# Hybrid conv encoder step: the last down product in three stretches of tokens instead of two, and VectorE instead of GpSimd for the output rows of a finished stretch

## The chip, the cores and the metric

One core of a Trainium2 chip runs one program. The metric is the device time of the whole program in microseconds, as the median of several runs. The profile below is of one execution of the same program.

## The reference

An encoder layer with two half-step feed-forward networks around a pair of gated convolution branches, and a norm at the end, over 512 + 64 tokens of 1024 features. What matters here is its last part, cut to the lines that it consists of:

```python
def rms_norm(x, g):
    xf = x.astype(jnp.float32)
    y = xf * lax.rsqrt(jnp.mean(xf * xf, axis=-1, keepdims=True) + EPS)
    return (y * g.astype(jnp.float32)).astype(x.dtype)

def swiglu_ffn(x, w_gate_up, w_down):
    gate, up = jnp.split(x @ w_gate_up, 2, axis=-1)
    return (jax.nn.silu(gate) * up) @ w_down
...
    x = x + 0.5 * swiglu_ffn(rms_norm(x, ffn2_norm), ffn2_w_gate_up, ffn2_w_down)
...
y_prompt = rms_norm(xp, final_norm)
y_sample = rms_norm(xs, final_norm)
```

Everything is float32. The hidden width of the feed-forward network is 2816.

## The kernel before

Features lie on the 128 partitions and the 576 tokens on the free axis, so the residual `X` is 8 tiles of 128 x 576. Every product is made of three matmuls in fp32r, TensorE's one-pass form of float32: a weight tile and an operand are each split into a high part (rounded to fp32r) and a low part (the rest), and high x high, high x low and low x high are added up in PSUM (`mm`). Each matmul has its own 128 x 128 weights. Up to the last stage a product covers the tokens in two halves of 288.

Weights come from HBM by a stream of DMAs on SP's queue into `raw` tiles. ScalarE rounds them to the high part and writes its negative, and a DMA with accumulation on GpSimd's queue (POOL) adds the raw tile to that, which leaves the low part.

The instructions of TensorE, VectorE, ScalarE and GpSimd stay in the order in which the program calls them (`Ordered`, whose line 81 stands at nearly every row of the profile). So the order of the Python code is the order on each engine, and an engine that waits holds up all that stands behind it.

The hidden features are worked off in four groups of tiles. The down product of the last group is the program's last: six hidden tiles, hence 6 x 3 = 18 matmuls for each stretch of tokens and each of the eight feature tiles `j`. The first three feature tiles are done over all tokens. For the other five (`LATE`) the tokens are taken in stretches (`LATE_SPANS`): all five tiles over the first stretch, then all five over the second, with the same weights. After each product

- VectorE adds half of it to `X[j]` (`x<-mm,x` in the profile),
- ScalarE squares the new `X[j]` (`tmp<-x`), and VectorE adds the square to `acc` (`fsum`),
- ScalarE writes `X[j]` times the gain of the final norm into an output tile (`gained`; `g<-x,gains`); an output tile `ys[q]` holds two feature tiles.

When all five tiles of a stretch are done, `rstd` makes the reciprocal root: two matmuls with a matrix of ones add up `acc` over the partitions, VectorE scales the sum (`tmp<-mm`), ScalarE takes the root (`r<-tmp`), and three VectorE steps refine it (`tmp<-r`, `tmp<-tmp,tmp`, `r<-tmp,r`). For a stretch that is not the last, `fsum.gather` first splits `acc` into two fp32r parts; for the last, the two matmuls run in plain float32, on `acc` and on the last square. Then each output tile is multiplied by the root and sent to HBM (`put`).

Before, the first stretch has 304 tokens and the second 272. The root of the first stretch is made right behind the second stretch's first product, and its four multiplies are GpSimd's, while TensorE goes on with the second stretch; those of the second stretch are VectorE's, at the end of the program. Output tiles come from a pool of eight buffers (`gtile`), PSUM tiles from a pool of four (`psum2`).

Of the kernel before, what the change touches and what calls it, by code (L numbers as in the profile page):

```python
# [11 lines left out]
ALU = mybir.AluOpType  # L12

P = 128
D = 1024
KT = D // P
# [5 lines left out]
T = SEQ + DSEQ  # L22
# [20 lines left out]
LATE = range(3, KT)  # L43

HALVES = ((0, H), (H, T))
LATE_SPANS = (((0, 304),), ((304, T),))

FIRST_KS = (1, 1, 2, 2, 2)
WARM = 10
# [55 lines left out]
def tile_encoder_step(  # L105
# [6 lines left out]
    nc = tc.nc  # L112
    pe, dve, sca, pool = (
        Ordered(tc, e, c)
        for e, c in (
            (nc.tensor, pe_cost), (nc.vector, dve_cost), (nc.scalar, None), (nc.gpsimd, None)
        )
    )
# [12 lines left out]
    def nm(s):  # L131
        uid[0] += 1
        return f"{s}_{uid[0]}"
# [4 lines left out]
    def gtile(dt=F32, n=LB):  # L138
        return conv.tile([P, 640], dt, tag="g", name=nm("g"))[:, :n]
# [7 lines left out]
    def ttile(dt=F32):  # L147
        return tmp.tile([P, T], dt, tag="tmp", name=nm("tmp"))

    def psum2():  # L150
        return mmps.tile([P, 2, 512], F32, tag="mm", name=nm("mm"))
# [26 lines left out]
    def table(func):  # L178

        t = cpool.tile([P, 1], F32, tag="table", name=nm("table"))  # L180
        sca.activation(t, eps, func)
# [6 lines left out]
    def par(j, r, n=1):  # L188
        return gains[:, r : r + n, j] if r < R_CA else prm[:, r - R_CA : r - R_CA + n, j]
# [198 lines left out]
    def mm(ps, w, kk, xs, first, last, spans=HALVES, six=SIX):  # L388


        (whi, wlo), (xh, xl) = w, xs
        parts = ((whi, xh), (whi, xl), (wlo, xh))
        for n, s in six:
            if s < len(spans):
                (a, b), (i, e) = parts[n], spans[s]
                pe.matmul(
                    ps[:, s, : e - i], a[:, kk, :], b[:, i:e],
                    start=first and n == 0, stop=last and n == 2,
                )

    def chunks(name):

        got = []
        for n in plan[name]:
            w = ws.get(n)
            got += [(w, kk) for kk in range(ws.units[n][1])]
        return got
# [19 lines left out]
    def product(name, xs, then=None, order=None, got=None):  # L427

        if name in early:
            return early.pop(name)[:, :, :H]  # L430
        ps = psum2()
        if order or got:
            got = got or chunks(name)
            for n, k in enumerate(order or range(len(xs))):
                mm(ps, *got[k], xs[k], n == 0, n == len(xs) - 1)
        else:
            k = 0
            for n in plan[name]:
                w = ws.get(n)
                for kk in range(ws.units[n][1]):  # L440
                    mm(ps, w, kk, xs[k], k == 0, k == len(xs) - 1)
                    k += 1
        take()
        if then is None:
            dve.time = max(dve.time, pe.time)
            return ps[:, :, :H]
        fill()
        behind.append((pe.time, lambda: then(ps[:, :, :H])))

    def both(names, xs):  # L450

        ps = [psum2() for _ in names]
        ws_ = [chunks(name) for name in names]
        for k in range(len(xs)):
            for p, w in zip(ps, ws_):
                mm(p, *w[k], xs[k], k == 0, k == len(xs) - 1)
        return [p[:, :, :H] for p in ps]
# [78 lines left out]
            n = spans[0][1] - spans[0][0]  # L536
            return p[:, :, :n] if len(spans) == 2 else p[:, 0, :n]

    def rstd(total, spans=HALVES):

        a, t = ttile(), ttile()
        r = rpool.tile([P, T], F32, tag="r", name=nm("r"), bufs=2)
        tot = total.total(spans)
        span = slice(spans[0][0], spans[-1][1])
        shaped = halves if len(spans) == 2 else (lambda v: v)
        a, t, y = a[:, span], t[:, span], r[:, span]
        dve.tensor_scalar(shaped(a), tot, 1.0 / D, EPS, op0=ALU.mult, op1=ALU.add)
        sca.activation(y, a, AF.Abs_reciprocal_sqrt)
        dve.scalar_tensor_tensor(t, y, -0.5, y, op0=ALU.mult, op1=ALU.mult)
        dve.tensor_tensor(t, t, a, op=ALU.mult)  # L550
        dve.scalar_tensor_tensor(y, t, 1.5, y, op0=ALU.add, op1=ALU.mult)
        return r
# [151 lines left out]
    table(AF.Abs_reciprocal_sqrt)  # L704
    multiply(7)
    R1 = rstd(ss)
    table(AF.Silu)
    forms1.combine(0)
# [10 lines left out]
    def update(j, ps, R=None):  # L719

        x = halves(X[j])
        if R is None:
            dve.scalar_tensor_tensor(x, ps, 0.5, x, op0=ALU.mult, op1=ALU.add)
        else:
            t = halves(ttile())
            dve.scalar_tensor_tensor(t, ps, 0.5, halves(R), op0=ALU.mult, op1=ALU.mult)
            dve.tensor_tensor(x, x, t, op=ALU.add)

    def ffn(f, xg, sums, finish, forms, R=None, todo=()):
# [5 lines left out]
        def plain(i, hs):  # L735
# [4 lines left out]
            if R is None:  # L740
                R = rstd(sums)
# [220 lines left out]
    for j in range(KT):  # L962
        raw = j < RAW_J
        xs = xg if raw else xn
        product(("p", 4, j), xs, gate_b(j, raw))
        if R is None:
            R = rstd(ss)
        if raw:
            xn.extend(scaled(range(3 * j, min(KT, 3 * j + 3)), R))
        product(("p", 3, j), xs, value_b(j))  # L970
# [165 lines left out]
    def finish2(g, hs):  # L1136
        fsum = Sum()
        table(AF.Abs_reciprocal_sqrt)
        ps = both([("f2", "d", g, j) for j in range(2)], hs)
        for j in range(LATE[0]):  # L1140
            update(j, ps[j] if j < 2 else product(("f2", "d", g, j), hs))
            fsum.square(X[j])
            fsum.add(dve)
        late = {}
        ydst = y.rearrange("(q a p) t -> q p a t", a=2, p=P)

        ys = {}

        def gained(j, span):

            n = span.stop - span.start
            q, a = j // 2, j % 2
            if a == 0:
                ys[q] = gtile(n=2 * n).rearrange("p (a n) -> p a n", a=2)
            sca.activation(ys[q][:, a, :], X[j][:, span], AF.Copy, scale=par(j, R_NF))

        def put(spans, engine, queues):

            i, e = spans[0]
            RF = rstd(fsum, spans)[:, i:e].unsqueeze(1).broadcast_to((P, 2, e - i))  # L1160
            for q in range(KT // 2):
                engine.tensor_tensor(ys[q], ys[q], RF, op=ALU.mult)
                queues[q % 2].dma_start(ydst[q, :, :, i:e], ys[q])

        for n, spans in enumerate(LATE_SPANS):
            i, e = spans[0]
            span = slice(i, e)
            fsum.n = LATE[0]
            for j in LATE:
                if n == 0:  # L1170
                    late[j] = chunks(("f2", "d", g, j))
                ps = psum2()
                for k, (w, kk) in enumerate(late[j]):
                    mm(ps, w, kk, hs[k], k == 0, k == len(hs) - 1, spans)
                xj = X[j][:, span]
                dve.scalar_tensor_tensor(
                    xj, ps[:, 0, : e - i], 0.5, xj, op0=ALU.mult, op1=ALU.add
                )
                if n > 0 and j == LATE[0]:
                    put(LATE_SPANS[0], pool, (nc.sync, nc.sync))  # L1180
                    fsum.terms = None
                fsum.square(X[j], span=span)
                fsum.add(dve)
                if j == LATE[0]:
                    for b in range(LATE[0]):
                        gained(b, span)
                gained(j, span)
            if n == 0:
                fsum.gather(span)
        put(spans, dve, (nc.sync, sca))  # L1190

    ffn("f2", xg, ss, finish2, forms)


# [43 lines left out]
```

## Time and profile before

| | |
|---|---|
| runs shown, median | 1304.97 us (1304.52 to 1306.55, three runs) |
| profiled execution | 1305.16 us, of which the span of its instructions is 1303.4 us |
| TensorE busy | 1287.0 us, 99% of the span |
| VectorE, ScalarE, GpSimd busy | 68%, 59%, 30% of the span |
| chain that ended last | TensorE 96%, VectorE 2%, ScalarE 1%, DMA 1% |
| mean granted TensorE clock | 0.995 |

In the rows of the profile, PE is TensorE's matmuls, PEld its weight loads, DVE VectorE, ACT ScalarE, POOL GpSimd, SP SyncE. A row of the timeline has the start and the duration in us, the engine, the line, the operation, what is written and read, the shape, a count, and in brackets the idle time before it with who ended it. A row of a group has the count, then the busy time in us and the mean of one in ns, then the idle time before. A row that merges several instructions runs from the first one's start to the last one's end. Matmuls are pipelined: one of them is shown longer than the time after which the next one starts. Plain float32 matmuls and their loads show twice for each one in the program.

### The profile page before, as it was taken

How to read it: one execution, taken by the hardware profiler on the slowest of the kernel's cores; microseconds unless marked ns; L12 is line 12 of the kernel's file. 1: busy time of each engine (PE TensorE's matmuls, PEld its weight loads, DVE VectorE, ACT ScalarE, POOL GpSimd, SP SyncE). 2: the span in 40 equal slices, each digit the busy share in tenths (PEclk: the TensorE clock that was granted, in tenths of full speed). 3: DMA queues.
4: the chain of work that ended last, by engine and by line, in shares of the span. 5: the costliest groups of instructions: out<-in, count | busy, mean ns of one | idle time of the engine just before them, and what ended most of it. 6: DMA issues, size and time to landing. Idle time of an engine off the chain costs nothing.

```text
span 1303.4 us, 25701 instructions
## 1 busy us (share of the span) xinstructions
PE 1287.0 (99%) x9754; PEld 1284.8 (99%) x9754; DVE 890.4 (68%) x1463; ACT 771.5 (59%) x1365; POOL 388.7 (30%) x487
## 2 busy tenths in 40 slices
PE   9899999999999999999999999999999999999997
PEld 9899999999999999999999999999999999999996
DVE  6748758747945899888885260336967848847955
ACT  7755646645677654555544684457665655654664
POOL 0142332332242554333321322222142141241233
PEclk9899999999999999999999999999999999999999
DMA  6596796796798898878885978776687696796784
GB/s 195 122 181 157 143 192 151 163 197 144 157 189 183 164 213 175 168 170 176 172 170 124 198 159 177 158 162 143 139 172 170 148 195 151 162 204 137 161 177 108
DMA packets 287804, 215.91 MB, mean 166 GB/s; under 512 B 15552, under 2 KB 250048, under 8 KB 287680
## 3 DMA queue, kind: packets, MB, share of 16 engines
q0 software_dynamic: 59472, 97.81, 45.9%
q1 hardware_dynamic: 226336, 115.33, 31.2%
q8 instruction: 77, 1.26, 0.4%
q10 hardware_dynamic: 1872, 1.13, 0.3%
q14 instruction: 47, 0.39, 0.1%
HBM read 113.81 MB, written 2.62 MB: 89 GB/s over the span
## 4 chain that ended last, share of the span: by engine, by line
PE 96%; DVE 2%; ACT 1%; DMA 1%; issue 0%; DVEq 0%; SPq 0%; ACTq 0%
PE mm L81 96%; DVE acc L81 0%; DVE tmp L81 0%; DMA raw<-in_ffn_w_gate_up_dram 0%; ACT tmp L81 0%; ACT act L81 0%; DMA x<-in_x_dram 0%; DVE act L81 0%; ACT w L81 0%; DVE g L81 0%; DVE x L81 0%; ACT L81 0%; DVEq L1228 0%; DVE r L81 0%; ACT u L81 0%
## 5 line engine op out<-in xcount | busy, mean ns | idle before, releaser
L81 PE MATMUL mm<-act,u 128*128 128x288 f32 x4686 | 660.5, 294 | 0.0
L81 PEld LDWEIGHTS mm<-act,u 128*128 128x128 f32 x4686 | 630.9, 188 | 0.2 <-DMA u<-raw 0.2
L81 PE MATMUL mm<-act,g 128*128 128x288 f32 x2778 | 401.6, 295 | 5.4 <-DVE tmp L81 5.4
L81 PEld LDWEIGHTS mm<-act,g 128*128 128x128 f32 x2778 | 380.1, 189 | 5.9 <-ACT g L81 4.8
L81 PE MATMUL mm<-act,act 128*128 128x288 f32 (+2 forms) x2244 | 306.2, 293 | 0.6 <-ACT act L81 0.6
L81 PEld LDWEIGHTS mm<-act,act 128*128 128x128 f32 x2244 | 297.4, 188 | 0.8 <-ACT act L81 0.8
L81 POOL DMA_DIRECT2D u<-raw x200 | 174.8, 874 | 371.5 <-ACT u L81 306.4
L81 ACT CAST u<-raw 128x512 fp32r<-128x512 f32 (+2 forms) x203 | 116.2, 572 | 158.8 <-PE mm L81 128.2
L81 POOL DMA_DIRECT2D g<-raw x123 | 107.7, 875 | 315.5 <-ACT g L81 226.2
L81 DVE SCALAR_TENSOR_TENSOR w<-g,prm,w 128x606 f32<-128x606 f32 x232 | 179.3, 843 | 1.4 <-ACT w L81 1.4
L81 DVE TENSOR_TENSOR tmp<-mm,tmp 128x288 f32<-128x288 f32 (+1 forms) x239 | 107.7, 459 | 76.8 <-PE mm L81 58.9
L81 POOL DMA_DIRECT2D act<-raw x90 | 78.0, 866 | 198.7 <-ACT act L81 191.7
L81 ACT ACTIVATE u<-u 128x512 fp32r<-128x512 f32 (+2 forms) x200 | 118.6, 593 | 6.3
L81 ACT CAST g<-raw 128x512 fp32r<-128x512 f32 (+2 forms) x126 | 68.9, 547 | 41.2 <-DMA raw<-in_ffn_w_down_dram 19.3
L81 DVE SCALAR_TENSOR_TENSOR tmp<-mm,r 128x576 f32<-128x576 f32 x48 | 36.3, 757 | 76.5 <-PE mm L81 76.5
L81 ACT CAST u<-w 128x512 fp32r<-128x512 f32 x79 | 48.9, 619 | 63.5 <-DVE w L81 56.3
L81 ACT CAST g<-w 128x512 fp32r<-128x512 f32 x77 | 47.7, 620 | 59.7 <-DVE w L81 53.6
L81 ACT CAST act<-tmp 128x576 fp32r<-128x576 f32 x84 | 56.7, 675 | 42.3 <-DVE tmp L81 40.8
L81 DVE TENSOR_TENSOR act<-tmp,act 128x576 fp32r<-128x576 f32 x84 | 62.2, 755 | 19.3 <-ACT act L81 17.9
L81 ACT ACTIVATE g<-g 128x512 fp32r<-128x512 f32 (+2 forms) x123 | 69.8, 568 | 3.9
L81 ACT CAST act<-raw 128x512 fp32r<-128x512 f32 (+3 forms) x94 | 55.6, 592 | 10.7 <-PE mm L81 7.5
L81 DVE TENSOR_TENSOR w<-raw,raw 128x512 f32<-128x512 f32 x78 | 53.4, 685 | 12.3 <-DMA raw<-in_ffn_w_gate_up_dram 12.3
(89 smaller groups left out, 808.2 us busy)
## 6 DMA issues: line engine op xcount, KB each, us to landing
raw<-in_ffn_w_gate_up_dram SPq DMA_DIRECT2D x171, 256.0 KB, 3.4
u<-raw POOLq DMA_DIRECT2D x141, 256.0 KB, 4.0
raw<-in_w_in_dram SPq DMA_DIRECT2D x112, 256.0 KB, 3.9
act<-raw POOLq DMA_DIRECT2D x80, 256.0 KB, 4.0
raw<-in_ffn_w_down_dram SPq DMA_DIRECT2D x96, 192.0 KB, 3.5
g<-raw POOLq DMA_DIRECT2D x64, 256.0 KB, 3.9
u<-raw POOLq DMA_DIRECT2D x43, 192.0 KB, 4.7
g<-raw POOLq DMA_DIRECT2D x43, 192.0 KB, 4.5
```

The costliest lines, as they stand in the source:

```text
L81: return self.tc.keep_in_program_order(fn(*args, **kwargs))
```

## The change

The tokens of the last five products are taken in three stretches of 272, 208 and 96. The multiplies by the root are VectorE's in every stretch. `put` returns them as a list of steps, one for each output tile; they are taken one by one behind VectorE's steps of the next stretch. The root of a finished stretch is made one product later for each stretch (`j == LATE[n]`): behind the second product of the second stretch, and behind the third one of the third. Steps that are left over when the last root is made are put between its scaling and its refinement (`meanwhile`).

```diff
-LATE_SPANS = (((0, 304),), ((304, T),))
+LATE_SPANS = (((0, 272),), ((272, 480),), ((480, T),))
...
-    def rstd(total, spans=HALVES):
+    def rstd(total, spans=HALVES, meanwhile=()):
...
         sca.activation(y, a, AF.Abs_reciprocal_sqrt)
+        for step in meanwhile:
+            step()
         dve.scalar_tensor_tensor(t, y, -0.5, y, op0=ALU.mult, op1=ALU.mult)
...
-        def put(spans, engine, queues):
+        def put(spans, ys, queues, meanwhile=()):
 
             i, e = spans[0]
-            RF = rstd(fsum, spans)[:, i:e].unsqueeze(1).broadcast_to((P, 2, e - i))
-            for q in range(KT // 2):
-                engine.tensor_tensor(ys[q], ys[q], RF, op=ALU.mult)
-                queues[q % 2].dma_start(ydst[q, :, :, i:e], ys[q])
+            RF = rstd(fsum, spans, meanwhile)[:, i:e].unsqueeze(1).broadcast_to((P, 2, e - i))
+
+            def rows(q, v):
+                dve.tensor_tensor(v, v, RF, op=ALU.mult)
+                queues[q % 2].dma_start(ydst[q, :, :, i:e], v)
+
+            return [(lambda q=q, v=v: rows(q, v)) for q, v in ys.items()]
+
+        puts = []
 
         for n, spans in enumerate(LATE_SPANS):
             i, e = spans[0]
             span = slice(i, e)
             fsum.n = LATE[0]
+            done = dict(ys)
             for j in LATE:
...
-                if n > 0 and j == LATE[0]:
-                    put(LATE_SPANS[0], pool, (nc.sync, nc.sync))
+                if n > 0 and j == LATE[n]:
+                    puts.extend(put(LATE_SPANS[n - 1], done, (nc.sync, nc.sync)))
                     fsum.terms = None
+                elif puts and j == LATE[-1]:
+                    puts.pop(0)()
                 fsum.square(X[j], span=span)
                 fsum.add(dve)
...
                 gained(j, span)
-            if n == 0:
+                if puts and j > LATE[n]:
+                    puts.pop(0)()
+            if n < len(LATE_SPANS) - 1:
                 fsum.gather(span)
-        put(spans, dve, (nc.sync, sca))
+        for rows in put(spans, ys, (nc.sync, sca), puts):
+            rows()
```

On TensorE, where the root of the first stretch is made: `mm_...` are PSUM tiles, `act_...` weight parts and hidden features, `ones_r` the matrix of ones and `tmp_...` the two parts of the gathered squares. Before, at the end of the second stretch's first product:

```order
L81 MATMUL mm_16225<-act_15910,act_15924 128x272
L81 MATMUL mm_16225<-act_15908,act_15925 128x272
L81 MATMUL mm_16248<-tmp_16220,ones_r 128x304
L81 MATMUL mm_16248<-tmp_16221,ones_r 128x304
L81 MATMUL mm_16273<-act_15180,act_15931 128x272
L81 MATMUL mm_16273<-act_15198,act_15931 128x272
```

Now, at the end of its second product:

```order
L81 MATMUL mm_16254<-act_15910,act_15938 128x208
L81 MATMUL mm_16254<-act_15908,act_15939 128x208
L81 MATMUL mm_16277<-tmp_16220,ones_r 128x272
L81 MATMUL mm_16277<-tmp_16221,ones_r 128x272
L81 MATMUL mm_16290<-act_15180,act_16024 128x208
L81 MATMUL mm_16290<-act_15198,act_16024 128x208
```

The pair has moved behind one more product of 18 matmuls, and all rows around it have 208 columns where they had 272.

On VectorE, the end of the program: `x_94` is the last feature tile, `r_...` the root, `g_...` the output tiles. Before:

```order
L81 SCALAR_TENSOR_TENSOR x_94<-mm_16347,x_94 128x272
L81 TENSOR_SCALAR tmp_16370<-mm_16373 128x272
L81 SCALAR_TENSOR_TENSOR tmp_16371<-r_16372 128x272
L81 TENSOR_TENSOR tmp_16371<-tmp_16371,tmp_16370 128x272
L81 SCALAR_TENSOR_TENSOR r_16372<-tmp_16371,r_16372 128x272
L81 TENSOR_TENSOR g_16267<-g_16267,r_16372 128x544
```

Now:

```order
L81 TENSOR_TENSOR acc_15912<-acc_15912,tmp_16484 128x96
L81 TENSOR_TENSOR g_16248<-g_16248,r_16451 128x416
L81 SCALAR_TENSOR_TENSOR x_94<-mm_16491,x_94 128x96
L81 TENSOR_TENSOR g_16251<-g_16251,r_16451 128x416
L81 TENSOR_TENSOR g_16288<-g_16288,r_16451 128x416
L81 TENSOR_SCALAR tmp_16518<-mm_16521 128x96
L81 TENSOR_TENSOR g_16339<-g_16339,r_16451 128x416
L81 SCALAR_TENSOR_TENSOR tmp_16519<-r_16520 128x96
L81 TENSOR_TENSOR tmp_16519<-tmp_16519,tmp_16518 128x96
L81 SCALAR_TENSOR_TENSOR r_16520<-tmp_16519,r_16520 128x96
L81 TENSOR_TENSOR g_16398<-g_16398,r_16520 128x192
```

Four multiplies of the second stretch stand around the last update: one ahead of it, two between it and the scaling, one between the scaling and the first step of refinement. The steps of the last stretch have 96 columns, and its output tiles 192.

## The prediction

> **What bounds the kernel now.** I read the page's shares and chain first, then the chain and the timeline of the last 40 us, then the groups of instructions there by shape, since all that the change touches lies behind 1267.96 us.
>
> ```profile
> span 1303.4 us, 25701 instructions
> PE 1287.0 (99%) x9754; PEld 1284.8 (99%) x9754; DVE 890.4 (68%) x1463; ACT 771.5 (59%) x1365; POOL 388.7 (30%) x487
> PE 96%; DVE 2%; ACT 1%; DMA 1%; issue 0%; DVEq 0%; SPq 0%; ACTq 0%
> ```
>
> TensorE is 96% of the chain, so a matmul added anywhere lengthens the kernel, and only the part behind the last product is held by other engines. In the timeline of TensorE's matmuls and weight loads (start, duration, operation, count, idle time and who ended it) the last products are these:
>
> ```profile
> 1267.96 14.84 PE L81 MATMUL mm<-act,act 128*128 128x304 f32 x108
> 1282.64 0.85 PE L81 MATMUL mm<-tmp,ones_r 128*128 128x304 f32 x2
> 1283.08 0.19 PEld L81 LDWEIGHTS mm<-tmp,ones_r 128*128 128x128 f32 x1 [0.33 <-DVE tmp L81]
> 1283.18 9.20 PEld L81 LDWEIGHTS mm<-act,act 128*128 128x128 f32 x72
> 1283.32 9.28 PE L81 MATMUL mm<-act,act 128*128 128x272 f32 x72
> L81 PE MATMUL mm<-act,act 128*128 128x272 f32 x90 | 11.7, 289 | 0.0
> ```
>
> The 72 matmuls of 272 columns take 9.28 us; less the 0.29 of a single one, over 71 steps, that is one every 126.6 ns. The x108 row holds the 90 of 304 columns and the 18 of the second stretch's first product: (14.84 - 0.29 - 17 x 0.1266) / 90 = 137.8 ns for one of 304. Between 1282.64 and 1283.32 the two small matmuls of the norm's sum cost 0.68 us, 0.33 of it a wait for VectorE. The last product ends at 1283.32 + 9.28 = 1292.60. What follows is a serial chain:
>
> ```profile
> 1292.77 0.43 DVE L81 SCALAR_TENSOR_TENSOR x<-mm,x 128x272 f32<-128x272 f32 x1
> 1293.29 0.43 ACT L81 ACTIVATE tmp<-x 128x272 f32<-128x272 f32 x1 [1.60 <-DVE x L81]
> 1293.77 0.73 PE L81 MATMUL mm<-tmp,ones 128*128 128x272 f32 x2
> 1294.53 0.44 DVE L81 TENSOR_SCALAR tmp<-mm 128x272 f32<-128x272 f32 x1 [1.34 <-PE mm L81]
> 1295.01 0.43 ACT L81 ACTIVATE r<-tmp 128x272 f32<-128x272 f32 x1 [0.88 <-DVE tmp L81]
> 1295.47 0.44 DVE L81 SCALAR_TENSOR_TENSOR tmp<-r 128x272 f32<-128x272 f32 x1 [0.49 <-ACT r L81]
> 1296.42 0.44 DVE L81 SCALAR_TENSOR_TENSOR r<-tmp,r 128x272 f32<-128x272 f32 x1
> 1296.90 2.63 DVE L81 TENSOR_TENSOR g<-g,r 128x544 f32<-128x544 f32 x4
> 1298.35 1.65 ACTq L81 DMA_DIRECT2D out_y_dram<-g  x2
> ```
>
> From 1292.60 to the span's end it is 10.8 us. Nearly every step of it has the last stretch's 272 tokens as its width; 3.87 us lie behind the last row multiply (1296.90 + 2.63 = 1299.53): issue and landing of the last DMA and the program's end.
>
> **The change part by part.** A third stretch means 90 more matmuls, each with a weight load of its own, and the columns of all stretches together stay 576. What counts is the price of a narrow matmul, which no row shows for these products: the narrowest fp32r one has 272 columns. Weight loads show themselves where TensorE had been idle, or where the matmul is short:
>
> ```profile
> 1283.18 0.19 PEld L81 LDWEIGHTS mm<-act,act 128*128 128x128 f32 x1
> 1292.89 0.30 PEld L81 LDWEIGHTS mm<-acc,ones 128*128 128x128 f32 x2 [0.51 <-DVE acc L81]
> 1293.77 0.30 PEld L81 LDWEIGHTS mm<-tmp,ones 128*128 128x128 f32 x2 [0.57 <-ACT tmp L81]
> 4.46 0.41 PEld L81 LDWEIGHTS mm<-ones 128*128 128x128 f32 x3
> ```
>
> The fp32r load of 1283.08 is followed by the next one at 1283.18, 0.10 us later; two plain loads of 0.19 each take 0.30 together, so they start 0.11 apart. In each case I read the second load's start as the moment when the first set of weights is in place and its matmul begins, with room for one set ahead; a set then takes 0.10 to 0.11 us. The last loads of the warm-up, ahead of matmuls of 128 columns, step by (0.41 - 0.19) / 2 = 0.11 as well. So a matmul with new weights would not follow its forerunner in less than about 0.11 us, however few its columns: at 272 the load hides behind the 126.6 ns of stream, at 208 just no longer, at 96 not at all. The lower bound is 0.104 for 208 columns and 0.065 for 96, by carrying on the line from 304 to 272 (0.35 ns a column); the upper bound is the 126.6 ns of 272. I take 0.11 for both, by the warm-up's steady row, which is nearest: there too each matmul has a load of its own.
>
> [...]
>
> Term 1, first stretch 304 to 272: 90 x (0.1378 - 0.1266) = -1.0.
>
> Term 2, a new wait in it. The last product (j = 7) needs the low parts of its weights, which POOL's accumulating DMAs bring:
>
> ```profile
> 1274.93 1.82 POOL L81 DMA_DIRECT2D act<-raw  x2 [2.21 <-ACT act L81]
> DMA to landing us min/median/max: 3.0/3.1/3.3
> ```
>
> The first of the two lands at 1274.93 + 3.0 = 1277.93, the second, issued 0.96 later, at 1279.2. Before, the first low part is the 75th matmul's, at 1267.96 + 74 x 0.1378 = 1278.16, with its load one step earlier, so 0.1 us of slack. Now that load stands ready at 1267.96 + 73 x 0.1266 = 1277.2, and the DMA comes only some 0.14 earlier (ScalarE, busy all that time, saves 4 x 0.03 on the gained rows, 537 against 508 ns, and 0.02 on the square, 452 against 430, rows below). It waits 0.6, and the second unit, nine matmuls on, another 0.1: +0.7 (from 0 to 0.9).
>
> Term 3, the second stretch 272 to 208: 90 x (0.11 - 0.1266) = -1.5. Term 4, the third stretch: 90 x 0.11 = +9.9. Term 5, the norm's sums: 0.68 before; now two pairs, each one product later, when VectorE has long made their operands, so 0.25 + 0.22, which is -0.2.
>
> Term 6, the tail. Durations by shape in the last stage (busy, mean ns):
>
> ```profile
> L81 DVE SCALAR_TENSOR_TENSOR x<-mm,x 128x576 f32<-128x576 f32 x3 | 2.3, 758 | 6.0 <-PE mm L81 6.0
> L81 DVE SCALAR_TENSOR_TENSOR x<-mm,x 128x272 f32<-128x272 f32 x5 | 2.2, 436 | 0.7 <-PE mm L81 0.6
> L81 DVE TENSOR_TENSOR g<-g,r 128x544 f32<-128x544 f32 x4 | 2.6, 719 | 0.0
> L81 ACT ACTIVATE tmp<-x 128x576 f32<-128x576 f32 x2 | 1.4, 688 | 2.1 <-DVE x L81 2.1
> L81 ACT ACTIVATE tmp<-x 128x304 f32<-128x304 f32 x5 | 2.3, 452 | 2.9 <-DVE x L81 2.9
> L81 ACT ACTIVATE tmp<-x 128x272 f32<-128x272 f32 x5 | 2.1, 430 | 4.3 <-DVE x L81 4.3
> L81 ACT ACTIVATE g<-x,gains 128x304 f32<-128x304 f32 x8 | 4.0, 537 | 0.0
> L81 ACT ACTIVATE g<-x,gains 128x272 f32<-128x272 f32 x8 | 3.8, 508 | 0.0
> L81 DVE TENSOR_TENSOR acc<-acc,tmp 128x272 f32<-128x272 f32 x4 | 3.4, 857 | 1.6 <-ACT tmp L81 1.6
> L81 POOL TENSOR_TENSOR g<-g,r 128x608 f32<-128x608 f32 x4 | 6.4, 1616 | 9.4 <-DVE r L81 9.4
> out_y_dram<-g SPq DMA_DIRECT2D x4, 304.0 KB, 2.3
> out_y_dram<-g ACTq DMA_DIRECT2D x2, 272.0 KB, 2.6
> out_hist_dram<-hst ACTq DMA_DIRECT2D x1, 256.0 KB, 3.4
> ```
>
> VectorE costs some 1.05 ns a column and 0.15 us besides (758 and 436 ns for 576 and 272; 719 for 544), ScalarE 0.85 and 0.20. At 96 columns that is 0.25 and 0.28. The five serial VectorE steps before the rows save 0.18 each (-0.9), the two of ScalarE 0.15 each (-0.3), the sum's two matmuls about 0.26. The four row multiplies go from 544 to 192 elements: 0.35 for one, 0.27 from start to start (they overlap by 0.08: 2.63 is three steps of 0.64 and 0.72), 1.2 in place of 2.63, -1.4. The update x of the last product started 0.17 behind the matmul, since VectorE was in a slowed sum (857 ns in place of some 440 while POOL multiplies): -0.1, as POOL has no multiplies left. Against that, three row multiplies of the second stretch (416 elements, 0.59, 0.51 apart) stand in this chain, two ahead of the scaling and one ahead of the next step; their covers are the square with the sum (0.8) and the reciprocal root (0.35), so +0.07 and +0.08. The last DMA has 96 KB for 272: I take 0.4 off the 3.87; a store of short runs took 3.4 us in the trace (the history's row, in 256-byte pieces) against the 2.6 of the output's, so the bounds are -0.8 and +0.8. Sum -3.3.
>
> [...]
>
> Of what is moved: POOL's four multiplies (6.4 us) ended nothing on the chain, and VectorE, with 18 x 0.11 = 2 us a product, takes them on (0.72 each) without lateness. SP gets four more output DMAs; nothing but output stands in its queue by then. The third stretch's scaled rows reuse the first stretch's buffers and wait for its DMAs (2.3 us to landing): ScalarE needs the third tile two products, 4 us, behind the update after which VectorE multiplies it, so it is free by then.
>
> Sum: -1.0 + 0.7 - 1.5 + 9.9 - 0.2 - 3.3 = +4.6 us on the profiled execution, whose own time is 1305.16 (span 1303.4). It stands 0.2 above the median of the runs, 1304.97, so I predict 1309.6.
>
> **The rivals.** Not slower: the loads do not bind, and a narrow matmul costs what the line through 304 and 272 gives. Then terms 3 and 4 are 90 x (0.104 - 0.1266) + 90 x 0.065 = 3.8 in place of 8.4, and the sum is 0.0. VectorE then limits the third stretch: between its start and the last update it has one update of 208, two multiplies of 544, a sum and a rest of 208, the norm's four steps, eight steps of 96 and a multiply of 416, by the widths above some 7.4 us with its waits, against 6.1 of TensorE, so up to +1.3: 1305 to 1306.3. For it speaks that between 304 and 272 the step falls with the columns; against it the loads' 0.10 to 0.11 us. It decides from a mean step of 0.099 on downward: 2.0 us less, spread over 180 matmuls, bring the 4.6 to the 2.6 that a measurement tells from nothing. [...]
>
> Much slower: below some width fp32r falls back to the passes of plain fp32. The plain pair above streams 272 columns in 0.73 - 0.11 (load) - 0.16 (drain: 0.29 less 0.127) = 0.46, four times 113 ns. With that, 0.36 for 208 columns and 0.17 for 96: 47.7 us in place of 19.8, 1337.5. Nothing in the trace speaks for it but that no fp32r product narrower than 272 was run; against it, the one-pass price at 272 and 304 is a stream that shrinks with the columns, with no sign of a step.
>
> **How the numbers follow.** Loads bind: 0.72, and its own range is 1308 to 1312.6 (0.108 a matmul and no wait of term 2 give 1308.5, a last DMA 0.4 better 1308.1; 0.12 a matmul and the slow last DMA 1312.6). Line through the widths: 0.10. Fall back to passes: 0.12. A sum better than all of these, by a tail or a stage that I misread: 0.06. Some 0.2% (2.6 us) is what a measurement can tell from no change. Slower by more: 0.68 + 0.12 + 0.03 = 0.83; within: 0.13; faster: 0.04. The range reaches down to the line's 1305 and up to 1312.6.
>
> **What would show it.** Matmuls of 208 and 96 columns at the same step, near 0.11, with loads as near each other; a wait of TensorE for a DMA of act<-raw near 1277.5; both norm pairs without a wait; the last product's end near 1300.4; from there to the end 7.5 us; POOL without multiplies, VectorE's sums of 208 near 0.38. I am wrong if the 96-column step is well under 0.1 or near 0.17, or if VectorE is late for TensorE's last product.

## The result and the profile after

The changed kernel takes 1314.5 us, the median of six runs (1309.74 to 1315.8), against 1305.3 for the kernel before in the same series: a ratio of 1.0063, 95% interval 1.0051 to 1.0075. The direction is as forecast, the size is twice the 4.6 us, and the time lies above the range of 1305.0 to 1312.6.

The six runs form two groups, and the clock that TensorE was granted tells them apart: 1309.74 and 1310.63 us with a mean clock of 0.996, and 1314.43, 1314.57, 1315.44 and 1315.8 with 0.991. The profile after is of the first of the short ones (span 1307.9), and for that run nearly every sign that the prediction named is there. Its timeline of TensorE's matmuls (PE) and weight loads (PEld), and of GpSimd:

```profile
1266.49 9.78 PE L81 MATMUL mm<-act,act 128*128 128x272 f32 x74
1273.74 2.30 PEld L81 LDWEIGHTS mm<-act,act 128*128 128x128 f32 x18 [0.29 <-DMA act<-raw]
1274.21 1.82 POOL L81 DMA_DIRECT2D act<-raw  x2 [2.07 <-ACT act L81]
1277.25 6.37 PE L81 MATMUL mm<-act,act 128*128 128x272 f32 x52 [0.98 <-DMA act<-raw]
1283.46 0.43 PE L81 MATMUL mm<-tmp,ones_r 128*128 128x272 f32 x2
1283.60 12.15 PEld L81 LDWEIGHTS mm<-act,act 128*128 128x128 f32 x108
1295.71 0.44 PE L81 MATMUL mm<-tmp,ones_r 128*128 128x208 f32 x2
1295.99 4.37 PE L81 MATMUL mm<-act,act 128*128 128x96 f32 x36
```

The x108 loads belong to three products of 208 columns and three of 96: (12.15 - 0.19) / 107 = 0.112 us for one, where the prediction had 0.11. The first stretch's weight loads wait 0.29 and 1.20 us for the low weights (0.98 of the second shows on the matmuls), and both pairs of the norm's sum pass without a wait. The chain of waits at its end:

```profile
1277.25 23.12 PE mm L81 x200
1300.38 0.02 issue
1300.40 0.27 DVE x L81
1300.69 0.29 ACT tmp L81
1301.03 0.76 PE mm L81 x2
1301.98 0.58 DVE g L81
1303.35 0.36 DVE g L81
```

TensorE ends at 1300.38, and the tail from there to the span's end (1307.9) is 7.5 us. VectorE's rows by shape (busy, mean ns) have the predicted lengths too:

```profile
L81 DVE TENSOR_TENSOR acc<-acc,tmp 128x208 f32<-128x208 f32 x5 | 1.9, 372 | 1.5 <-ACT tmp L81 1.5
L81 DVE SCALAR_TENSOR_TENSOR x<-mm,x 128x96 f32<-128x96 f32 x5 | 1.3, 255 | 2.1 <-PE mm L81 2.1
L81 DVE TENSOR_TENSOR g<-g,r 128x192 f32<-128x192 f32 x4 | 1.2, 352 | 0.0
```

What is new stands in the busy time by stretch (us, then PE, PEld, DVE, ACT, POOL, and the granted clock as the third number from the end): TensorE's clock is halved in the third stretch, just before the last matmuls.

```profile
1290.00:1299.60 9.60, 9.60 (x88) 9.60 (x88) 5.99 (x19) 4.27 (x15) 0.00 (x0) 1.00 0.29 96
1299.80:1302.00 2.20, 1.81 (x7) 1.33 (x6) 1.45 (x5) 0.55 (x2) 0.00 (x0) 0.50 0.31 97
```

In this run that costs some tenths of a microsecond: the last two products take 4.37 us, against 4.18 where the clock holds (the padded run below). The experiments ask whether the same thing, earlier, makes the long runs.

### The profile page after: what moved, and what is told of

Same layout as the page of the kernel before. It is cut to its first block, busy times and chain, and to the rows that moved or that the text cites. A ratio compares the mean times of both kernels' runs of the same rounds, so it can differ in the third digit from the quotient of the medians.

```text
span 1307.9 us, 25926 instructions
## 1 busy us (share of the span) xinstructions
PE 1294.6 (99%) x9846; PEld 1292.9 (99%) x9846; DVE 893.5 (68%) x1486; ACT 774.2 (59%) x1380; POOL 383.2 (29%) x483
## 4 chain that ended last, share of the span: by engine, by line
PE 96%; DVE 1%; ACT 1%; DMA 1%; issue 1%; POOL 0%; SPq 0%; DVEq 0%; POOLq 0%; ACTq 0%
PE mm L81 96%; DMA raw<-in_ffn_w_gate_up_dram 0%; ACT act L81 0%; DVE tmp L81 0%; DVE acc L81 0%; DMA x<-in_x_dram 0%; DVE act L81 0%; DMA act<-raw 0%; ACT tmp L81 0%; ACT w L81 0%; DVE g L81 0%; ACT L81 0%; ACT u L81 0%; ACT g L81 0%; DVE x L81 0%
## 5 line engine op out<-in xcount | busy, mean ns | idle before, releaser
L81 PE MATMUL mm<-act,act 128*128 128x288 f32 (+3 forms) x2334 | 314.9, 291 | 1.1 <-DMA act<-raw 1.0
L81 PEld LDWEIGHTS mm<-act,act 128*128 128x128 f32 x2334 | 305.7, 188 | 1.8 <-DMA act<-raw 1.5
```

What stands on the lines that cost most here:

```text
L81: return self.tc.keep_in_program_order(fn(*args, **kwargs))
```

## The experiments

Theory L: the weight loads set the pace of narrow matmuls. Theory G: in the third stretch TensorE streams so little of the time that its clock is halved. Rival W: the wait for the weights makes the long runs. Rival F: a narrow matmul has a fixed price that has nothing to do with its load. The series shared 17 to 19 runs of the kernel before, with medians of 1305.33 to 1305.64; one of them, of 2577 us, stands apart.

**The changed kernel again** (no edit).

> The changed kernel once more, for the spread of its runs. [...] Then the runs lie between 1309 and 1316 us, the longer ones with a mean granted clock near 0.991 against 0.996, and a profile of such a run shows the clock at half from inside the third stretch on, with 96-column matmuls there 0.22 us apart. Theory W (weights): the length comes from TensorE's wait for the low weights in the first stretch, which took 1.5 us in the one profile and may take 5 more in other runs; then the clock is the same in all runs and a long run shows the wait.

Measured: 1315.23 us (1314.64 to 1316.16, five runs), ratio 1.0076 (1.0064 to 1.0088), mean clock 0.990 or 0.991 in all five. The profile, of such a run, shows busy time by stretch and TensorE's rows:

```profile
1290.20:1294.40 4.20, 4.20 (x40) 4.20 (x40) 3.04 (x9) 2.10 (x8) 0.00 (x0) 1.00 0.70 231
1294.40:1305.60 11.20, 11.20 (x55) 11.20 (x54) 3.36 (x11) 2.16 (x9) 0.00 (x0) 0.50 0.07 20
1277.68 6.16 PEld L81 LDWEIGHTS mm<-act,act 128*128 128x128 f32 x52 [1.22 <-DMA act<-raw]
1297.98 7.80 PEld L81 LDWEIGHTS mm<-act,act 128*128 128x128 f32 x36
L81 PEld LDWEIGHTS mm<-act,act 128*128 128x128 f32 x15 | 3.3, 330 | 0.0
```

From 1294.4 on the clock is at half, some 4 us into the third stretch, and the loads come every (7.80 - 0.33) / 35 = 0.213 us. The 11.2 us at half clock hold 54 loads, which at 0.112 would take 6.0: 5.2 us are lost there. The wait of the loads for the weights is 1.22 us, no longer than in the short run (0.29 and 1.20). G's signs are all there (half clock from inside the third stretch, 0.213 us a matmul, a mean clock of 0.990 or 0.991); W's is not.

**The same number of matmuls and loads, but more columns streamed.**

```diff
-                    mm(ps, w, kk, hs[k], k == 0, k == len(hs) - 1, spans)
+                    mm(ps, w, kk, hs[k], k == 0, k == len(hs) - 1, ((i - pad, e),))
...
-                    xj, ps[:, 0, : e - i], 0.5, xj, op0=ALU.mult, op1=ALU.add
+                    xj, ps[:, 0, pad : pad + e - i], 0.5, xj, op0=ALU.mult, op1=ALU.add
...
+            pad = 112 if n == 2 else 0
```

> Third stretch streams 208 columns (112 tokens of the second stretch over again, their results unused) instead of 96; all else as changed. [...] If narrow matmuls go at the pace of their loads, 208 columns cost the same 0.112 us as 96, so the time of a run whose clock holds stays 1309.5 to 1310.5. G: the clock is not halved before the last product's end in any run, all runs 1309 to 1311, about 4 us under the median of the changed kernel. W: the spread up to 1316 stays, since the wait for the weights is unchanged.

Measured: 1309.97 us (1309.07 to 1310.61, five runs), ratio 1.0036 (1.0024 to 1.0048), clock 0.996 or 0.997. More than twice the columns in the third stretch, and 5.3 us less. Its rows, with the wait for the weights still there (0.45 on the matmuls, 0.67 on their loads; 0.99 and 1.22 in the long run):

```profile
1277.08 6.38 PE L81 MATMUL mm<-act,act 128*128 128x272 f32 x52 [0.45 <-DMA act<-raw]
1283.56 12.21 PE L81 MATMUL mm<-act,act 128*128 128x208 f32 x108
1295.83 4.18 PE L81 MATMUL mm<-act,act 128*128 128x208 f32 x36
1290.00:1300.00 10.00, 10.00 (x92) 10.00 (x91) 5.91 (x18) 4.33 (x15) 0.00 (x0) 1.00 0.27 87
```

The 108 and the 36 matmuls, now all of 208 columns, take as long as the mixed ones of the short run (12.16 and 4.37, the last with its end at half clock). So 112 columns more cost nothing, and the clock stays full to the last product. The padding changes only the streamed columns, so it shows that the clock went with them here (G), and half of L: at 0.112 us a load, the stream of 208 columns cost no more than that of 96.

**With 128 and 160 columns** (the same edit with `pad` 32 and 64: so many tokens are streamed over again, unused), to find where the gate lies.

> [...] L: the step stays 0.112. Theory G (clock gate by the share of time in which columns stream) with a point of one half: the clock is halved before the last product's end, runs up to 1316. G with a point between 0.36 and 0.48: all runs 1309 to 1311.

> [...] L: the step stays 0.112. G with a point of one half or lower: all runs 1309 to 1311, mean clock 0.996. G with a point above 0.6: the clock is halved there, runs up to 1316.

Measured: 1309.71 us (1308.9 to 1310.15) and 1309.6 (1309.28 to 1310.7), ratios 1.0036 (1.0022 to 1.005) and 1.0037 (1.0024 to 1.0049), five runs each, clock 0.995 or more in all. Of the run with 128 columns:

```profile
1295.61 4.10 PEld L81 LDWEIGHTS mm<-act,act 128*128 128x128 f32 x36
1290.00:1299.60 9.60, 9.60 (x89) 9.60 (x87) 5.81 (x18) 4.31 (x15) 0.00 (x0) 1.00 0.27 89
```

The step is 0.112 again ((4.10 - 0.19) / 35). So 128 columns every 112 ns held the clock in all five runs, and 96 every 112 ns did not. How long a column streams can be bounded by rows of the kernel before: between 0.35 ns (the difference of the steps at 304 and 272) and 0.45 (137.8 / 304, as if nothing else were in the step). That is 34 to 44 ns of stream for 96 columns, a share of 0.30 to 0.39, and 45 to 58 ns for 128, a share of 0.40 to 0.52. For 160 columns it is 56 to 72 ns, a share of 0.50 to 0.64. The points of 0.36, 0.48 and 0.6 that the expectations name were assumed: no run shows them, and the rows give these bounds alone. If the clock goes by this share, the point lies between those of 96 and 128 columns.

**Half the weight columns in the third stretch** (half of the features of the last 96 tokens go without the last group's product).

```diff
+                    if n == 2:
+                        (whi, wlo), (xh, xl) = w, hs[k]
+                        for m, (l, r) in enumerate(((whi, xh), (whi, xl), (wlo, xh))):
+                            pe.matmul(
+                                ps[:64, 0, : e - i], l[:, kk, :64], r[:, i:e],
...
+                rows = slice(0, 64 if n == 2 else P)
```

> In the third stretch each matmul loads 64 of the 128 weight columns, so half of the features of the last 96 tokens go without the last group's down product; number of matmuls, 96 streamed columns and all other steps stay. [...] Rival F (a fixed cost of some 0.11 us for every matmul, whatever it loads): the step stays 0.112, the clock is halved in the third stretch as in the changed kernel, 1314 to 1316.

Measured: 1308.23 us (1307.26 to 1309.33, eight runs), ratio 1.0023 (1.0013 to 1.0033), clock 0.994 to 0.997. TensorE's loads and matmuls:

```profile
1293.81 2.22 PEld L81 LDWEIGHTS mm<-act,act 128*64 128x64 f32 x36
1298.69 0.46 PE L81 MATMUL mm<-acc,ones 128*128 128x96 f32 x2 [2.53 <-DVE acc L81]
```

36 loads of 64 columns in 2.22 us are at most 0.062 each, against 0.112 of 128 (in the padded run 0.112 too): the price went with the columns of weights, so F falls. The edit also halves the rows that each matmul writes, and no run here tells the two apart; that it is the load (L) rests on the loads' row, which has no gap. The clock held in all eight runs although the matmuls had 96 columns: at 0.062 us each, 54 of them begin within 3.41 us, where 30 do at 0.112, so here the clock went with the columns in a time and not with the width.

Theory L had put the end 2.5 to 4 us before that of the padded third stretch, at 1306 to 1307.5 us, and the time missed this by 0.7 us and more: TensorE's products end about 1296.2, and then it waits 2.5 us for VectorE, whose chain is

```profile
1298.38 0.26 DVE acc L81
1298.63 0.50 DVE g L81
1299.14 0.16 DVE x L81
1299.30 0.90 DVE g L81 x2
1300.47 0.50 DVE g L81
```

So even with loads of half the time in the third stretch the three stretches lose 3 us (1308.23 against 1305.33), for VectorE has then too much to do beside it.

**Two stretches, with the rest of the change.**

```diff
-LATE_SPANS = (((0, 272),), ((272, 480),), ((480, T),))
+LATE_SPANS = (((0, 304),), ((304, T),))
```

> Two stretches of 304 and 272 as before, with the rest of the change: VectorE multiplies the first stretch's rows, root one product later. All theories: no narrow matmul, so no load-paced stage and no halved clock. Against the kernel before: 0.2 us less of waiting at the norm's sum, VectorE's sums no longer slowed, so 0 to 0.5 us faster, 1304.6 to 1305.3. If it is slower by over 1 us, VectorE's multiplies themselves are a cost that the prediction took for hidden.

Measured: median 1304.51 us (twelve runs, 1303.75 to 1305.35 but for one of 6352), ratio 0.9993 (0.9984 to 1.0002). The row multiplies on VectorE, the later root and GpSimd's relief cost nothing that shows and may bring a little; the loss comes with the cut into three.

**Three even stretches of 192.**

> Three stretches of 192 each. 270 matmuls of one width, each 0.112 us if the loads set the pace: 30.2 us against 31.5 in the changed kernel with its clock held (11.4 + 10.05 + 10.05), a tail of 192 tokens instead of 96 costs some 1.8 us (0.0186 us a token, from 3.3 us for 176), and the wait for the low weights grows by some 1 us, as the first stretch is over earlier. [...] W: a longer wait in the first stretch, spread as in the changed kernel or larger. [...]

Measured: 1310.58 us (1310.3 to 1311.84), ratio 1.0042 (1.003 to 1.0054). The matmuls, 270 of one width:

```profile
1284.52 12.22 PE L81 MATMUL mm<-act,act 128*128 128x192 f32 x108
1290.00:1300.00 10.00, 10.00 (x92) 10.00 (x91) 5.86 (x17) 4.88 (x15) 0.00 (x0) 1.00 0.21 66
```

12.22 us for 108, as with 208 columns and with 96 under full clock; the waits for the weights are 1.7 us of the loads' time, and yet no run is long, and the clock is 0.996 or 0.997 in all five. L holds, and so does G, by which more columns keep the clock; W falls a second time.

**Two stretches of 320 and 256.**

> Two stretches of 320 and 256 with VectorE's multiplies. [...] 1304.0 to 1304.5, 0.1% under the kernel before and just under the two stretches of 304 and 272. If the loads' pace already bound at 256, some 0.5 us more. The clock holds.

Measured: 1304.8 us (1303.8 to 1306.01, eleven runs), ratio 0.9998 (0.9989 to 1.0007). At 256 columns the load is still covered: the 54 loads of the second stretch give (6.57 - 0.19) / 53 = 0.120 us, which is more than 0.112. But what 16 tokens less of tail bring (an estimate: 3.3 us of term 6 for 176 tokens, hence 0.3) is not to be seen among runs that differ by 2.

```profile
1286.00 6.57 PEld L81 LDWEIGHTS mm<-act,act 128*128 128x128 f32 x54
```

**Earlier casts of the last weights, and the kernel before once more**, for the wait of the first stretch.

```diff
-                if n == 0:
+                if n == 0 and j not in late:
                     late[j] = chunks(("f2", "d", g, j))
...
+                if n == 0 and j == LATE[0]:
+                    late[j + 1] = chunks(("f2", "d", g, j + 1))
```

> Two stretches of 304 and 272 with VectorE's multiplies, and ScalarE's casts of the last tile's weights set ahead of the first square and the four gained rows (2.1 us of ScalarE's work) in the first stretch. If ScalarE's order makes the low parts late, TensorE's wait for them (0.7 to 0.9 us with two stretches) goes, and the time is 0.7 us lower than with two stretches alone: 1303.8. If the load of the raw tile is what comes late, ScalarE only waits for it at another place, and the time stays at 1304.5.

> The padded three stretches with the same earlier casts. The wait of TensorE in the first stretch is 0.5 to 1.2 us there. If it goes, 1309.0 to 1309.4 against 1309.97; the rest of the loss stays, being the loads' pace.

> The kernel before, for one more profile of its first stretch: whether TensorE's wait for the last low weights, absent from the one profile (slack 0.1 us), is there in another run. If the wait belongs to the narrower first stretch, none; if it varies from run to run with the arrival of the raw tiles, 0 to 0.9 us.

Measured: two stretches with early casts 1303.97 us, ratio 0.9992 (0.9983 to 1.0001); the padded three stretches with them 1309.09 us (1307.39 to 1311.24), ratio 1.0027 (1.0017 to 1.0037); the kernel before 1305.18 in one run. Rows of the two stretches without and with the early casts, of the padded kernel with them, and the wait in the kernel before (in total, times, longest):

```profile
1277.73 7.04 PE L81 MATMUL mm<-act,act 128*128 128x304 f32 x52 [0.69 <-DMA act<-raw]
```

```profile
1267.19 17.12 PE L81 MATMUL mm<-act,act 128*128 128x304 f32 x126
```

```profile
1268.53 15.77 PE L81 MATMUL mm<-act,act 128*128 128x272 f32 x126
```

```profile
PEld mm L81 <- DMA act<-raw: 0.2, 1, 0.2
```

With ScalarE's order changed the wait is gone in both profiles, as it should be if that order is the cause. In time the gain does not show: against the kernel before in the same series the ratios fell from 0.9993 to 0.9992 and from 1.0036 to 1.0027, within their intervals. The wait is not the narrower stretch's alone: at 304 columns the loads waited 0.2 us (the kernel before, again), 0.9 (two stretches) and 0 (the profile that I had), against 0.7 to 1.5 in the six profiles at 272 without early casts. No version is surely faster than the kernel before; the interval of the best one ends at 1.0001.

## Why the prediction was right or wrong

The mechanism that was put first, with its price, is what the runs show at full clock: narrow fp32r matmuls go at the pace of their loads (terms 3 and 4: 0.11 assumed, 0.112 measured at 96, 128, 160, 192 and 208 columns). Term 6 held: 7.5 us behind the last product, as forecast, and 7.3 in the padded run; the last outputs, in pieces of 384 bytes, landed after 1.9 and 2.0 us against 2.5 and 2.6 before, so the slow last DMA of the upper bound did not come. Term 5 held: no wait at either pair.

Term 2 was seen: 1.2 and 1.5 us of waiting in the loads of the two profiles of the changed kernel, for 0.7. I took one profile's arrival of the weights as fixed relative to TensorE; in the profile after, the stage began 1.47 us earlier than before (1266.49 for 1267.96) and the last DMAs only 0.72 earlier (1274.21 for 1274.93). As a difference of means the term fits better: 1.1 us in the six profiles at 272 columns, 0.4 in the three at 304.

That the last product of the short run ended at 1300.38, where the prediction had 1300.4, is in part luck: from the stage's start it took 33.9 us where the sum gave 32.5, and the earlier start made up for it.

The step that failed is the price of 0.11 us taken as the same for the whole third stretch, and with it the range, "0.12 a matmul and the slow last DMA 1312.6": both suppose TensorE's clock at full to the end. At half clock a matmul took 0.213. With the clock held to near the end or throughout, the kernel takes 1309.6 to 1310.6 (the two short runs, the medians with padding), near the 1309.6 of the prediction; the padding, which changes nothing but the streamed columns, is worth 5.3 us. In the series of the experiments the loss of 9.6 us (1315.23 against 1305.64) is therefore 5.5 for the cut into three less its shorter tail (1309.97 against 1304.51 with two stretches), 5.3 for the clock, and -1.1 for the rest of the change, which by its interval may also be nothing (5.46 + 5.26 - 1.13 = 9.59).

The trace of before shows half clock in the middle of the program once, with a gap to go with it: TensorE stood idle for 4.56 us, and the clock fell some 2 us into the gap, at the end of a stretch in which TensorE was busy for 1.35 of 3.42 us.

```profile
31.64:35.06 3.42, 1.35 (x11) 1.11 (x9) 1.47 (x3) 3.36 (x7) 0.00 (x0) 1.00 0.02 6
35.06:38.47 3.41, 0.92 (x4) 0.95 (x5) 3.03 (x5) 3.35 (x7) 1.01 (x1) 0.50 0.77 225
37.55 0.82 PE L81 MATMUL mm<-act,g 128*128 128x288 f32 x2 [4.56 <-DVE tmp L81]
```

No row of before shows it without a gap. But that full clock is not always granted stood there, and a share of 34 to 44 ns of stream in 0.11 us could be worked out beforehand (96 columns at 0.35 to 0.45 ns). As a rival, at twice the step, it would have been priced at up to 10 us: 90 x 0.11 for the whole third stretch.

Of the rivals, the fall back to the price of plain fp32 did not come at any width: the fp32r step was 0.112 us from 208 columns down to 96, against the 0.46 us that the prediction estimates for the stream of 272 columns in plain fp32. The one without binding loads would not have been faster either, as forecast: with loads of half the columns VectorE became the limit, and TensorE's 2.5 us of waiting for it is more than the 1.3 that the rival put on it.

## What to carry to other kernels

Before a product is cut into narrower pieces, compare the stream of one piece with the time of its weight load: from 256 columns on the load was hidden here, and from 208 on downward every matmul cost the same 0.112 us, so cutting off 96 tokens cost as much as cutting off 208. Where the loads bind, also work out how many columns stream in a time, since here a matmul row that was busy throughout still lost half the clock (2880 columns in 3.41 us lost it and 3200 kept it); streaming more columns than were needed cost nothing here, and it was worth 5.3 us. A change at the end of a kernel is best priced against several runs' arrival of the last weights, not one profile's.

## What was not expected of the hardware

TensorE's clock was halved although no matmul waited: the busy rows show it at 1.00 of the time with 96 columns every 112 ns, and 128 columns were enough to hold the clock in five runs of five. The times of the changes have a pattern: in the profiles before and after, the stretches between two changes of the clock last whole multiples of 3.413 us (before, it changes at 35.06, 41.88 and 1297.99: 2 and 368 times; after, at 36.80, 40.22 and 1299.73: once and 369 times). TensorE was not idle ahead of the change in the third stretch. Cut into windows of this length that end at the changes, the short run (three windows) and the long one (two) look the same but for the clock that follows:

```profile
1289.49:1292.91 3.42, 3.42 (x33) 3.42 (x33) 2.99 (x7) 1.10 (x3) 0.00 (x0) 1.00 0.72 238
1292.91:1296.32 3.41, 3.41 (x33) 3.41 (x32) 1.16 (x5) 1.80 (x7) 0.00 (x0) 1.00 0.22 76
1296.32:1299.73 3.41, 3.41 (x33) 3.41 (x32) 2.46 (x8) 1.36 (x5) 0.00 (x0) 1.00 0.02 5
1291.01:1294.42 3.41, 3.41 (x33) 3.41 (x32) 2.25 (x7) 1.93 (x8) 0.00 (x0) 1.00 0.74 245
1294.42:1297.84 3.42, 3.42 (x18) 3.42 (x18) 0.39 (x2) 0.78 (x4) 0.00 (x0) 0.50 0.00 0
```

What differs is the columns of the matmuls that begin in a window. The first holds two of 208 and 29 of 96, the second 29 of 96 and the pair of 208 of the norm's sum: 3200 columns each, and the clock stayed. The third holds 30 of 96, which is 2880, and the fourth, of 96 alone at 0.112 us each, some 30 as well (3.41 / 0.112); half clock followed on both. Over all such windows of the traces before and after, leaving out those with plain float32 matmuls and those without any matmul, the two at full clock with 2880 columns or fewer (2304 in the gap of before, and the 2880) were followed by half clock, and none of the 749 with 3200 or more. So in these two traces the clock went by how many columns began in a window, and at 2880 it fell although no matmul waited.

By this I also explain which of the two a run gets. The clock falls early, some 4 us into the third stretch, when a window fits between its start and the norm's pair, which are 5.9 us apart (1289.8 to 1295.7); otherwise the pair's columns carry it over, and it falls at the very end. By these lengths, and if the windows begin anywhere alike from run to run, which no run shows, I estimate that (5.9 - 3.4) / 3.4, some three runs in four, fall early; four of six did in the first series and five of five in the second. Only one run of each kind was profiled, so this is worked out and not shown run by run.
